# Weight transfers of the plain projections issued by GpSimd instead of SyncE, up to the last one in the gates' stage

## The chip, the cores and the metric

The kernel runs on one core of a Trainium2 chip. The metric is the device time of one execution, in microseconds (us). The engines of the core are named as in the profile: PE (TensorE, matrix products; PEld is its weight load), DVE (VectorE), ACT (ScalarE), POOL (GpSimd) and SP (SyncE). Each has its own queue of instructions and works through it in order. A DMA is put on the way by an instruction in the queue of one engine (in this kernel nearly always SP's, "SPq" in the profile) and then carried out by 16 DMA engines; the profile's DMA rows name the engine that issued it.

## The reference

One layer of a hybrid encoder block in float32, batch 1, 1024 tokens, width 1024. Cut to what matters:

```python
h = rms_norm(x)
proj = h @ w_in                      # q, k, v, r and gate codes of GLA; q, k, v of SWA; two branch gates
A = gla(q, k, v, r, gates) @ w_o_gla # gated linear attention, both directions, 4 heads, chunks
B = swa(q, k, v, sinks) @ w_o_swa    # windowed attention, 8 heads on 2 KV heads, blocks of 128
x = x + (sigmoid(gate_a) * A + sigmoid(gate_b) * B) @ w_out
h2 = rms_norm(x)
gate, up = split(h2 @ w_ffn_in)
x = x + (silu(gate) * up) @ w_ffn_out
```

## The kernel before, in words

Every product is made at nearly full float32 precision from operands that are split in two: a value's high part is its rounding to a shorter format (`h`, made by ACT), its low part what is left (`l`, a subtraction by DVE). A product then takes three matmuls: high by high, high by low, low by high. In the profile the split parts of the weights are `wh` and `wl`, those of the normalised input `xh` and `xl`, raw weights `wr`; accumulators of dense products are `mm`, those of the attention's small products `ch`.

A "unit" is a 128x512 piece of a weight, 256 KB. `wunit` loads it raw into `wr` (4 buffers), lets ACT make `wh` and DVE make `wl` (5 buffers each). The plain projections (all of `w_in` that is used as it stands: `w_f` for outputs with features on the partitions, `w_t` for outputs with tokens there) are generators of dense matmuls; each takes its units with `next_unit`, which keeps two more units ahead (`AHEAD = 2`) of the one in use. Half of the tokens are worked off in a first pass: `wkeep` loads a unit of `w_t`, splits it and stores the split parts to DRAM (for n < 2 only the low part, otherwise both), and `wagain` loads them again for the other half of the tokens: for n < 2 the raw unit, of which ACT makes `wh` anew, and the low part; otherwise both parts.

The order of work on PE is written out by hand. The attention's steps (gates, decays, scores, outputs of GLA; later scores and outputs of SWA) are set in slots, and `fill(n)` puts n dense matmuls between them, so that PE has work while a chain of small operations goes through ACT and DVE. The tables `GF` and `SF` say how many for each slot. The order on ACT, DVE, SP and POOL is not written out: a scheduler makes it, from the program's dependences and its own estimates of when each instruction can begin. So a change in one queue changes the order in the others.

Stages, by the profile's time: a start with the load of x, its split and the sums of the norm (to about 36 us); GLA with the projections filled in (to about 375 us); SWA likewise (to about 560 us); the products of the later layers, in which sums of quarters of the matrices are used (to the end). In the third of these the branch gates' projections are made in pairs (`pair_open`, `pair_T1`, ...), which begins while the last plain units are worked off. Sums of other weights (`w_ob`, `w_out`) are made by `prep` steps between GLA's slots: DVE adds two raw pieces `xn`, loaded by SP at line 618, and the sums (`bs...`, `wo...`) are stored to DRAM by SP at line 117.

Other names that the steps below use: `st` is a stage from which SP stores a projection's result (lines 152 and 237); `qk` and `vr` are reloads of q, k and v for a GLA chunk; `G` are gates (ACT lines 461 to 483, DVE lines 462 to 485); `th` and `tl` the split state of GLA (ACT line 557, DVE line 558); `ac` the split sum of squares of the norm (ACT line 133, DVE line 135), made of `acc` (DVE line 354); `sql` the low part of SWA's queries (line 833); `pl` the low part of its probabilities (line 890).

Of the kernel before, what the change touches and what calls it, by code (L numbers as in the profile page):

```python
# [8 lines left out]
F32 = mybir.dt.float32  # L9
# [21 lines left out]
def body(tc, i, out):  # L31
    nc = tc.nc
    with ExitStack() as root:
# [8 lines left out]
        def nm(s):  # L42
            uid[0] += 1
            return f"{s}_{uid[0]}"
# [13 lines left out]
        def load_const(pool, name, src, shape, dt=F32):  # L58
            t = pool.tile(list(shape), dt, tag=name, name=name)
            nc.sync.dma_start(out=t, in_=src)  # L60
            return t

        def wunit(src, n=512):
            raw = wp.tile([P, n], F32, tag="wr", name=nm("wr"), bufs=4)
            nc.sync.dma_start(out=raw, in_=src)
            h = wp.tile([P, n], FR, tag="wh", name=nm("wh"), bufs=5)
            nc.scalar.activation(h, raw, AF.Copy)  # L67
            l = wp.tile([P, n], FR, tag="wl", name=nm("wl"), bufs=5)
            nc.vector.tensor_tensor(l, raw, h.bitcast(F32), op=ALU.subtract)  # L69
            return h, l  # L70
# [96 lines left out]
        def wkeep(n, k):  # L167
            h, l = wunit(i["w_t"][n, k])
            kept[n, k] = []
            for v, q in ((h, "h"), (l, "l"))[n < 2:]:  # L170
                d = dram.tile([P, 512], F32, tag=f"w{q}{n}_{k}", name=f"w{q}{n}_{k}")
                nc.sync.dma_start(out=d, in_=v.bitcast(F32))
                kept[n, k].append(d)
            return h, l

        def wagain(n, k):
            r = []
            if n < 2:
                raw = wp.tile([P, 512], F32, tag="wr", name=nm("wr"), bufs=4)
                nc.sync.dma_start(out=raw, in_=i["w_t"][n, k])  # L180
                r.append(wp.tile([P, 512], FR, tag="wh", name=nm("wh"), bufs=5))
                nc.scalar.activation(r[0], raw, AF.Copy)
            for d, tag in zip(kept[n, k], ("wh", "wl")[n < 2:]):
                t = wp.tile([P, 512], FR, tag=tag, name=nm(tag), bufs=5)
                nc.sync.dma_start(out=t.bitcast(F32), in_=d)
                r.append(t)
            return r

# [84 lines left out]
        def fill(n):  # L273

            while n > 0 and dense:
                try:
                    next(dense[0])
                    n -= 1
                except StopIteration:
                    dense.pop(0)  # L280
# [659 lines left out]
        def xpart(q, k):  # L940
            r = xn.tile([P, HT], F32, tag="xn", name=nm("xn"))
            nc.sync.dma_start(out=r, in_=scr[f"x{q}", k])
            pool, th, tl, d = homes[q]
            XT[q].append(xsplit(pool, th.format(k + d), tl.format(k + d), r))
# [4 lines left out]
        for n in range(2 * KT):  # L949
            t, g = divmod(n, 2)  # L950
# [10 lines left out]
        with tc.manual_schedule(engines={mybir.EngineType.PE}):  # L961
            for t, v in enumerate(todo):
# [5 lines left out]
                if a_scores in names:  # L968
                    pin = a_turn in names and t < 5
                    k = names.index(a_turn) if pin else max(j for j, f in enumerate(names) if f is a_scores)  # L970
# [56 lines left out]
        def pair_open(f):  # L1027
            nme, m, a, b = PAIRS[f]
            g = pend[f] = Chunk()
            p1 = tp.tile([P, HT], F32, tag="np", name=nm("np"), bufs=2)  # L1030
            nc.sync.dma_start(out=p1, in_=scr[f"{nme}{m}", "p1"])
            g.X = mmtile()
            nc.scalar.copy(g.X, p1)
            g.r11, g.r21 = rawload(i["w_f"][a, 0], True), rawload(i["w_f"][b, 0], True)
            g.s = comb(g.r21, rawload(i["w_f"][b, 1], False), ALU.add)
            g.w = wsplit(g.s, 512)
# [102 lines left out]
        with tc.manual_schedule(engines={mybir.EngineType.PE}):  # L1139
            homes["T2"] = tp, "t2h{}", "t2l{}", 0  # L1140
            for k in range(4):
                if k == 2:
                    pair_open(0)
                xpart("T2", k)
                fill(8)
            while plan:
                fill(4)
            pair_open(1)
            fill(1 << 30)
            for f in range(2):  # L1150
                pair_T1(f)
            for q in ("T3", "T4"):
                for k in range(4):
                    xpart(q, k)
            for j in range(0, len(PAIRS), 2):
                two = (j, j + 1)
                for step in (pair_T2, pair_22):
                    for f in two:
                        step(f)
                v = [pair_T3(f) for f in two]  # L1160
                if j + 2 == len(PAIRS):
                    for f in two:
                        pair_w4(f)
                for f in two:
                    with tc.issue_after(v[f - j].ins):
                        for q, k in STEPS[f]:
                            parts[q](k)
                if j + 2 < len(PAIRS):
                    for f in two:
                        pair_open(f + 2)  # L1170
                    for f in two:
                        pair_T1(f + 2)
                for f in two:
                    if j + 2 < len(PAIRS):
                        pair_w4(f)
                    pair_T4(f)
# [591 lines left out]
```

## Time and profile before

| | |
|---|---|
| median of 3 runs | 1604.43 us (1604.23 to 1604.52) |
| the profiled execution: time, span | 1605.86 us, 1604.0 us |
| mean granted clock of PE | 0.999 |
| DMA moved | 349.47 MB, mean 218 GB/s |
| DMAs issued by SP and by POOL | 1421 and 0 |

Each row of a busy window has the stretch in us, its length, then busy us (and instructions) of PE, PEld, DVE, ACT and POOL, PE's granted clock as a share of full speed, the busy share of the 16 DMA engines, and GB/s. Each row of a timeline has the start, the duration, the engine, the line, the operation with output and input, and in brackets the idle time before it with what ended it. Each row of waits has the engine and its instruction, what it waited for, the total in us, how often, and the longest.

### The profile page before, as it was taken

How to read it: one execution, taken by the hardware profiler on the slowest of the kernel's cores; microseconds unless marked ns; L12 is line 12 of the kernel's file. 1: busy time of each engine (PE TensorE's matmuls, PEld its weight loads, DVE VectorE, ACT ScalarE, POOL GpSimd, SP SyncE). 2: the span in 40 equal slices, each digit the busy share in tenths (PEclk: the TensorE clock that was granted, in tenths of full speed). 3: DMA queues.
4: the chain of work that ended last, by engine and by line, in shares of the span. 5: the costliest groups of instructions: out<-in, count | busy, mean ns of one | idle time of the engine just before them, and what ended most of it. 6: DMA issues, size and time to landing. Idle time of an engine off the chain costs nothing.

```text
span 1604.0 us, 23251 instructions
## 1 busy us (share of the span) xinstructions
PE 1590.2 (99%) x7484; PEld 1322.5 (82%) x7484; DVE 1247.0 (78%) x2358; ACT 932.7 (58%) x1912; POOL 0.2 (0%) x4
## 2 busy tenths in 40 slices
PE   9999999999999999999999999999999999999999
PEld 7878888888888788888888888888888888888887
DVE  8577898846899877876887988777777878689655
ACT  7555877864998744545664647844444444354442
POOL 0000000000000000000000000000000000000000
PEclk9999999999999999999999999999999999999999
DMA  8877877888554799878876767634344564695433
GB/s 266 287 260 250 272 260 253 283 281 292 182 158 155 235 298 300 266 254 268 273 248 191 233 213 222 201 113 151 112 150 153 192 201 162 205 333 172 151 99 118
DMA packets 223900, 349.47 MB, mean 218 GB/s; under 512 B 24255, under 2 KB 67135, under 8 KB 223778
## 3 DMA queue, kind: packets, MB, share of 16 engines
q1 hardware_dynamic: 223778, 347.99, 66.6%
q8 instruction: 59, 0.97, 0.2%
q14 instruction: 63, 0.52, 0.1%
HBM read 235.17 MB, written 112.73 MB: 217 GB/s over the span
## 4 chain that ended last, share of the span: by engine, by line
PE 77%; DVE 11%; DMA 6%; ACT 3%; issue 2%; SPq 1%; DVEq 0%; ACTq 0%
PE mm L1013 10%; PE mm L1014 10%; PE mm L1012 10%; PE mm L73 8%; PE mm L1606 7%; PE ch L1606 6%; PE ch L1012 5%; PE ch L1013 5%; PE ch L1014 5%; PE ch L73 5%; PE mm L261 4%; DMA wr<-in_w_f_dram 1%; PE ch L886 1%; DVE wl L69 1%; DMA gb<-gb 1%
## 5 line engine op out<-in xcount | busy, mean ns | idle before, releaser
L991 ACT ACTIVATE wh<-ws 128x512 fp32r<-128x512 f32 x164 | 103.2, 631 | 150.6 <-PE mm L1013 74.7
L73 PE MATMUL mm<-wh,xl 128*128 128x512 f32 x320 | 127.2, 398 | 0.0
L73 PE MATMUL mm<-wl,xh 128*128 128x512 f32 x320 | 127.2, 397 | 0.0
L73 PE MATMUL mm<-wh,xh 128*128 128x512 f32 x320 | 127.0, 397 | 0.1
L992 DVE TENSOR_TENSOR wl<-ws,wh 128x512 fp32r<-128x512 f32 x164 | 112.0, 686 | 11.0 <-ACT wh L991 10.8
L991 ACT ACTIVATE wh<-a 128x512 fp32r<-128x512 f32 x66 | 41.8, 634 | 89.6 <-PE ch L1606 42.2
L991 ACT ACTIVATE wh<-wr 128x512 fp32r<-128x512 f32 x96 | 60.0, 629 | 45.0 <-PE mm L1013 13.9
L69 DVE TENSOR_TENSOR wl<-wr,wh 128x512 fp32r<-128x512 f32 x98 | 66.9, 685 | 15.3 <-ACT wh L67 15.3
L992 DVE TENSOR_TENSOR wl<-wr,wh 128x512 fp32r<-128x512 f32 x96 | 65.5, 686 | 15.3 <-ACT wh L991 15.3
L992 DVE TENSOR_TENSOR wl<-a,wh 128x512 fp32r<-128x512 f32 x66 | 45.5, 690 | 40.5 <-ACT wh L991 40.2
L67 ACT ACTIVATE wh<-wr 128x512 fp32r<-128x512 f32 x98 | 61.2, 629 | 23.0 <-PE mm L73 8.3
L73 PEld LDWEIGHTS mm<-wh,xh 128*128 128x128 f32 x320 | 60.2, 188 | 10.7 <-DVE st L148 0.6
L1606 PE MATMUL mm<-hh,wl 128*128 128x512 f32 x176 | 68.6, 390 | 0.0
L1606 PE MATMUL mm<-hl,wh 128*128 128x512 f32 x176 | 68.6, 390 | 0.0
L1606 PE MATMUL mm<-hh,wh 128*128 128x512 f32 x176 | 68.5, 389 | 0.0
L73 PEld LDWEIGHTS mm<-wl,xh 128*128 128x128 f32 x320 | 60.2, 188 | 9.7 <-DMA wl<-wl 0.2
L73 PEld LDWEIGHTS mm<-wh,xl 128*128 128x128 f32 x320 | 60.3, 188 | 8.9
L1005 DVE TENSOR_TENSOR ws<-wr,wr 128x512 f32<-128x512 f32 x80 | 54.6, 686 | 12.1 <-DMA wr<-in_w_out_dram 5.5
L1573 DVE TENSOR_TENSOR hl<-hr,hh 128x512 fp32r<-128x512 f32 x77 | 52.8, 686 | 5.2 <-ACT hh L1572 5.0
L1012 PE MATMUL mm<-S0h,wh 128*128 128x512 f32 x136 | 52.9, 389 | 0.0
L1013 PE MATMUL mm<-S0l,wh 128*128 128x512 f32 x136 | 52.9, 389 | 0.0
L1014 PE MATMUL mm<-S0h,wl 128*128 128x512 f32 x136 | 52.9, 389 | 0.0
(445 smaller groups left out, 4947.4 us busy)
## 6 DMA issues: line engine op xcount, KB each, us to landing
wr<-in_w_fi_dram SPq DMA_DIRECT2D x110, 256.0 KB, 3.9
wr<-in_w_f_dram SPq DMA_DIRECT2D x96, 256.0 KB, 3.9
wl<-wl SPq DMA_DIRECT2D x80, 256.0 KB, 3.4
wr<-in_w_t_dram SPq DMA_DIRECT2D x56, 256.0 KB, 3.6
wh<-wh SPq DMA_DIRECT2D x48, 256.0 KB, 3.5
B<-c SPq DMA_DIRECT2D x44, 256.0 KB, 2.0
T<-st SPq DMA_DIRECT2D x44, 256.0 KB, 3.0
a<-in_w_fo_dram SPq DMA_DIRECT2D x44, 256.0 KB, 5.3
```

Source lines behind the costliest of these rows:

```text
L67: nc.scalar.activation(h, raw, AF.Copy)
L69: nc.vector.tensor_tensor(l, raw, h.bitcast(F32), op=ALU.subtract)
L73: nc.tensor.matmul(o, a, b, start=start, stop=stop)
L261: nc.tensor.matmul(Y[q], w[:, c], x, start=f0, stop=f1, skip_group_check=True)
L991: nc.scalar.activation(h, src, AF.Copy)
L992: nc.vector.tensor_tensor(l, src, h.bitcast(F32), op=ALU.subtract)
L1005: nc.vector.tensor_tensor(t, x, y, op=op)
L1012: nc.tensor.matmul(o, h[:, c], x[kk][0], start=start and kk == 0, stop=False, skip_group_check=True)
L1013: nc.tensor.matmul(o, h[:, c], x[kk][1], start=False, stop=False, skip_group_check=True)
L1014: nc.tensor.matmul(o, l[:, c], x[kk][0], start=False, stop=kk == nk - 1, skip_group_check=True)
L1573: nc.vector.tensor_tensor(l, r, h.bitcast(F32), op=ALU.subtract)
L1606: nc.tensor.matmul(ys[m], a[:, c], b, start=f0, stop=f1, skip_group_check=True)
```

## The change: a second queue for the weights

A list of one, `via`, holds the engine that issues the weight transfers of the three functions. It is GpSimd from the beginning; behind the last plain unit, when the plan of projections has been worked off in the gates' stage, it is set to SyncE. Up to there 220 DMAs of 256 KB are issued by GpSimd: 76 raw loads in `wunit`, 64 stores of split parts in `wkeep`, 16 raw loads and 64 loads of split parts in `wagain`. The later uses of `wunit` (22 units) are issued by SyncE as before. Nothing else is edited.

```diff
+        via = [nc.gpsimd]
+
         def wunit(src, n=512):
             raw = wp.tile([P, n], F32, tag="wr", name=nm("wr"), bufs=4)
-            nc.sync.dma_start(out=raw, in_=src)
+            via[0].dma_start(out=raw, in_=src)
...
             for v, q in ((h, "h"), (l, "l"))[n < 2:]:
                 d = dram.tile([P, 512], F32, tag=f"w{q}{n}_{k}", name=f"w{q}{n}_{k}")
-                nc.sync.dma_start(out=d, in_=v.bitcast(F32))
+                via[0].dma_start(out=d, in_=v.bitcast(F32))
...
             if n < 2:
                 raw = wp.tile([P, 512], F32, tag="wr", name=nm("wr"), bufs=4)
-                nc.sync.dma_start(out=raw, in_=i["w_t"][n, k])
+                via[0].dma_start(out=raw, in_=i["w_t"][n, k])
...
             for d, tag in zip(kept[n, k], ("wh", "wl")[n < 2:]):
                 t = wp.tile([P, 512], FR, tag=tag, name=nm(tag), bufs=5)
-                nc.sync.dma_start(out=t.bitcast(F32), in_=d)
+                via[0].dma_start(out=t.bitcast(F32), in_=d)
...
             while plan:
                 fill(4)
             pair_open(1)
             fill(1 << 30)
+            via[0] = nc.sync
```

PE's order is the same before and after. The orders of DVE, ACT and SP change in many places. Line numbers are those of each kernel; after the edit they are higher by 2 from line 63 on. In the rows a tile's name carries numbers of its own.

SP, before, in GLA's second chunk pair: weight loads (`wr`, L65) and reloads of v (`vr`) stand among the sums' loads and stores, and the load of `xn_203_1210` behind two stores of q.

```order
L65 DMA wr_208_1245<-in_w_f_dram 128x512
L117 DMA bs4l_1_1106<-pwl_176_1101 128x512
L618 DMA xn_202_1208<-in_w_ob_dram 128x512
L117 DMA woh_1_1202<-pwh_199_1198 128x512
L65 DMA wr_234_1353<-in_w_f_dram 128x512
L502 DMA vr_237_1370<-v0_4_959 128x256
L502 DMA vr_237_1370<-v0_5_991 128x256
L65 DMA wr_249_1417<-in_w_f_dram 128x512
L117 DMA wol_1_1204<-pwl_200_1199 128x512
L152 DMA q1_0_1174<-st_192_1175 128x512
L152 DMA q1_1_1178<-st_193_1179 128x512
L618 DMA xn_203_1210<-in_w_ob_dram 128x512
```

SP, after, at the same place:

```order
L119 DMA bs4h_1_1104<-pwh_175_1100 128x512
L504 DMA vr_237_1370<-v0_4_959 128x256
L504 DMA vr_237_1370<-v0_5_991 128x256
L119 DMA bs4l_1_1106<-pwl_176_1101 128x512
L119 DMA woh_1_1202<-pwh_199_1198 128x512
L620 DMA xn_202_1208<-in_w_ob_dram 128x512
L119 DMA wol_1_1204<-pwl_200_1199 128x512
L620 DMA xn_203_1210<-in_w_ob_dram 128x512
L154 DMA q1_0_1174<-st_192_1175 128x512
L154 DMA q1_1_1178<-st_193_1179 128x512
```

The three weight loads are gone, the reloads of v stand earlier, and `xn_203_1210` is loaded ahead of the stores of q.

POOL, after, the same weight units (POOL issues no DMA before):

```order
L67 DMA wr_137_941<-in_w_f_dram 128x512
L187 DMA wl_113_841<-wl0_5_595 128x512
L187 DMA wl_116_859<-wl0_6_646 128x512
L67 DMA wr_140_947<-in_w_f_dram 128x512
L67 DMA wr_154_1017<-in_w_f_dram 128x512
L187 DMA wl_136_927<-wl0_7_666 128x512
L67 DMA wr_177_1110<-in_w_f_dram 128x512
L67 DMA wr_196_1184<-in_w_f_dram 128x512
L67 DMA wr_208_1245<-in_w_f_dram 128x512
L67 DMA wr_234_1353<-in_w_f_dram 128x512
```

The loads of `w_f` that were spread over SP's rows stand here one behind the other, between the second loads of `w_t`.

DVE, before, at the end of the start: the sums of squares `acc`, the low part `ac1` of their total, and the subtractions `wl` of the first weights.

```order
L354 TENSOR_TENSOR acc_136<-acc_136,sq_24_356 128x1024
L354 TENSOR_TENSOR acc_136<-acc_136,sq_25_359 128x1024
L354 TENSOR_TENSOR acc_136<-acc_136,sq_26_362 128x512 x2
L740 TENSOR_SCALAR kg_505<-kg_505 128x128
L135 TENSOR_TENSOR ac1_394<-acc_136,ac0_393 128x512
L69 TENSOR_TENSOR wl_45_517<-wr_43_513,wh_44_515 128x512
L135 TENSOR_TENSOR ac1_394<-acc_136,ac0_393 128x512
L69 TENSOR_TENSOR wl_48_525<-wr_46_521,wh_47_523 128x512
L69 TENSOR_TENSOR wl_51_533<-wr_49_529,wh_50_531 128x512
```

DVE, after, at the same place:

```order
L356 TENSOR_TENSOR acc_136<-acc_136,sq_24_356 128x1024
L71 TENSOR_TENSOR wl_45_517<-wr_43_513,wh_44_515 128x512
L356 TENSOR_TENSOR acc_136<-acc_136,sq_25_359 128x1024
L71 TENSOR_TENSOR wl_48_525<-wr_46_521,wh_47_523 128x512
L356 TENSOR_TENSOR acc_136<-acc_136,sq_26_362 128x512 x2
L71 TENSOR_TENSOR wl_51_533<-wr_49_529,wh_50_531 128x512
L137 TENSOR_TENSOR ac1_394<-acc_136,ac0_393 128x512 x2
L71 TENSOR_TENSOR wl_54_541<-wr_52_537,wh_53_539 128x512
```

Three subtractions of weights, which stood between and behind the two of `ac1`, stand between the sums of squares and ahead of `ac1`.

## The prediction

> **What bounds the kernel now.** I read the busy table first, then the windows by stage, then the waits of TensorE, then the places of those waits on the engines that feed it. The profiled execution took 1605.86 us, 1604.0 us of it the span, so 1.86 us lie around the span; it stands 1.43 us above the median of 1604.43 us. The sum below is made against 1605.86 and then lowered by 1.43.
>
> The busy table (busy us, share of the span, instructions) and two windows (busy us of PE, PEld, DVE, ACT, POOL; granted clock; DMA share; GB/s), from the end of the start-up to the attention stage, and that stage:
>
> ```profile
> PE 1590.2 (99%) x7484; PEld 1322.5 (82%) x7484; DVE 1247.0 (78%) x2358; ACT 932.7 (58%) x1912; POOL 0.2 (0%) x4
> 36.00:375.00 339.00, 334.33 (x1783) 281.71 (x1782) 254.90 (x576) 229.84 (x594) 0.00 (x0) 0.99 0.81 269
> 375.00:560.00 185.00, 182.71 (x981) 155.49 (x980) 163.29 (x461) 155.37 (x381) 0.00 (x0) 1.00 0.63 198
> ```
>
> TensorE bounds it: 99% busy, and the diff adds or removes no matmul. In the stretch that the change touches TensorE is idle for 339 − 334.33 + 185 − 182.71 = 6.96 us. That, and a lowered clock, is all that can be gained. TensorE's waits between 20 and 560 us (us in total, times, longest):
>
> ```profile
> PE ch L73 <- DVE pl L890: 1.9, 3, 0.8
> PE ch L73 <- ACT th L557: 1.7, 2, 1.0
> PE ch L73 <- ACT ac L133: 1.0, 2, 0.5
> PE ch L73 <- DVE tl L558: 1.0, 2, 0.7
> PE ch L73 <- DVE ob L587: 0.6, 1, 0.6
> PE ch L73 <- DVE sh L527: 0.5, 1, 0.5
> PE mm L73 <- ACT st L236: 0.4, 1, 0.4
> PE ch L73 <- DVE sql L833: 0.4, 1, 0.4
> PE ch L73 <- DVE sl L528: 0.2, 1, 0.2
> ```
>
> No line names a weight: TensorE never waits for wh, wl or a DMA here. The waits, 7.7 us in all, are for chains of small operations on ScalarE and VectorE. So moving weight transfers can only help where a late weight holds up one of these chains.
>
> **The change part by part.** SyncE's queue of DMAs runs in order, and weight transfers stand and wait in it. Its own waits in the same stretch, for the three moved lines:
>
> ```profile
> SPq L65 <- DVE wl L69: 28.7, 17, 7.2
> SPq L185 <- PE mm L73: 21.7, 17, 3.8
> SPq L172 <- DVE wl L69: 14.7, 16, 4.2
> ```
>
> These 65.1 us, and the issue time of 220 DMAs, leave SyncE. What stands behind them there is activation loads and stores, among them the xn, qk and vr loads. Conversely the raw loads no longer stand behind SyncE's other waits. What that is worth is read at the places where TensorE waits.
>
> *The stall at 112 us.* On TensorE (start, duration, idle before it and its releaser), and the windows there:
>
> ```profile
> 113.41 0.39 PE L73 MATMUL ch<-th,q2f 128*128 128x256 f32 x1 [0.99 <-ACT th L557]
> 114.46 0.39 PE L73 MATMUL ch<-tl,q2f 128*128 128x256 f32 x1 [0.67 <-DVE tl L558]
> 112.00:115.00 3.00, 1.34 (x8) 0.93 (x7) 2.56 (x6) 2.73 (x9) 0.00 (x0) 1.00 0.70 237
> 115.00:119.00 4.00, 4.00 (x12) 3.11 (x11) 3.75 (x9) 2.05 (x6) 0.00 (x0) 0.58 0.47 168
> ```
>
> 0.99 + 0.67 = 1.66 us idle, and behind it a stretch of 4 us at a granted clock of 0.58: (1 − 0.58) × 4 = 1.68 us more. Together 3.34 us hang on one chain. The Trainium skill ("TensorE: Matmul & The Clock Gate", Part 1) says that the clock halves after an idle window of about 3.4 us and returns after as long a busy one; here the trace shows the drop behind an idle time of only 1.66 us, so the row decides. The chain, back from its end: VectorE and ScalarE, then SyncE:
>
> ```profile
> 110.52 0.69 DVE L622 TENSOR_TENSOR xn<-xn,xn 128x512 f32<-128x512 f32 x1 [1.99 <-DMA xn<-in_w_ob_dram]
> 111.13 0.16 DVE L480 TENSOR_SCALAR G<-G 128x2 f32<-128x2 f32 x1
> 112.84 0.51 ACT L557 ACTIVATE th<-pf,dec 128x256 fp32r<-128x256 f32 x1
> 103.80 1.25 SPq L152 DMA_DIRECT2D q<-st x2
> 105.10 0.44 SPq L618 DMA_DIRECT2D xn<-in_w_ob_dram x1
> ```
>
> VectorE is in order: the gate's G (L480) stands behind the sum L622, which idles 1.99 us for an xn load that SyncE issued at 105.10, behind two q stores that began at 103.80. In the new order that load stands ahead of the two stores. So it can be issued about 105.10 − 103.80 = 1.30 us sooner, more if its queue has drained (three weight loads and their waits are gone from the dozen rows before it). Of th's 0.99 and tl's 0.67, which lie on the same chain one behind the other, an advance of 1.66 removes both. 1.30 alone would leave 0.36; with what the drained queue adds I take the full 1.66 and with it the 1.68 of the clock: −3.34. The ends: nothing (the load waits for its buffer anyway) and −3.34.
>
> *The waits at 85 and 92 us.* ScalarE and then TensorE:
>
> ```profile
> ACT wh L67 <- DMA wr<-in_w_f_dram: 8.2, 4, 4.0
> 82.88 0.63 ACT L67 ACTIVATE wh<-wr 128x512 fp32r<-128x512 f32 x1 [4.00 <-DMA wr<-in_w_f_dram]
> 85.24 0.50 PE L73 MATMUL mm<-xh,wh 128*128 128x512 f32 x1 [0.36 <-ACT st L236]
> 90.49 0.63 ACT L67 ACTIVATE wh<-wr 128x512 fp32r<-128x512 f32 x1 [2.10 <-DMA wr<-in_w_f_dram]
> 92.30 0.39 PE L73 MATMUL ch<-tl,q2f 128*128 128x256 f32 x1 [0.30 <-DVE tl L558]
> ```
>
> ScalarE idled 4.00 and 2.10 us for a raw w_f load, and evictions (st) and th stood behind it. On GpSimd's queue these loads no longer stand behind SyncE's stores of wo and xn. If the load comes 0.4 us sooner, 0.36 + 0.30 = 0.66 us go. I take −0.66, one end; the other is +0.66, since a wh that comes sooner also takes ScalarE from something else.
>
> *The other waits* (pl, ob, sh, sql, sl: 3.6 us in all): VectorE's order around them is changed, with no clear direction. I take −0.5, a seventh of them, for casts that ScalarE has done earlier; ends −3.6 and +3.6.
>
> *The start.* Raw loads of w_t come to stand in an empty queue, so the first four are issued as soon as their buffers are free, beside the loads of x. The scheduler answers by moving their casts and subtractions ahead of the norm's sums. Window of the start, then VectorE and TensorE:
>
> ```profile
> 4.00:24.00 20.00, 20.00 (x88) 16.77 (x88) 17.13 (x25) 18.09 (x27) 0.00 (x0) 1.00 0.98 327
> 28.77 1.29 DVE L354 TENSOR_TENSOR acc<-acc,sq 128x512 f32<-128x512 f32 x2 [0.52 <-DVE acc L354]
> 30.16 0.69 DVE L135 TENSOR_TENSOR ac<-acc,ac 128x512 fp32r<-128x512 f32 x1
> 30.18 0.50 PE L73 MATMUL ch<-ac,onesr 128*128 128x512 f32 x1 [0.45 <-ACT ac L133]
> ```
>
> Two wl subtractions of about 0.6 us (as long as the ac of 0.69) come into the chain of acc, which has 0.52 us of slack: 2 × 0.6 − 0.52 = +0.7, on the matmul that already waits at 30.18. The ends: 0 (the wh arrives too late to be taken first, and the order costs only a wait) and +1.8 (three subtractions, no slack). As to the transfers: 4 × 0.262 MB at 327 GB/s are 3.2 us in a stretch where the DMA share is 0.98 and TensorE is busy for 20.00 of 20.00. ScalarE (18.09) has 1.9 us of room, so I take +0.3, ends 0 and +3.2.
>
> *GpSimd's issue.* No DMA is issued by GpSimd in this trace, so its price is unknown. SyncE's rows for the same shape, and the moved DMAs in the densest stretch, 260 to 380 us (count, KB each, us to landing):
>
> ```profile
> L185 SPq DMA_DIRECT2D wl<-wl x40: 319/423/667, 49.5 to 412.5; - x40
> wh<-wh SPq DMA_DIRECT2D x34, 256.0 KB, 3.2
> wl<-wl SPq DMA_DIRECT2D x33, 256.0 KB, 3.3
> wr<-in_w_t_dram SPq DMA_DIRECT2D x15, 256.0 KB, 3.1
> wr<-in_w_f_dram SPq DMA_DIRECT2D x4, 256.0 KB, 3.8
> 260.00:380.00 120.00, 119.33 (x650) 101.17 (x649) 83.72 (x212) 86.02 (x244) 0.00 (x0) 1.00 0.85 282
> ```
>
> 34 + 33 + 15 + 4 = 86 DMAs in 120 us, one each 1.40 us. At SyncE's 0.42 us GpSimd would be busy for 36 us of 120; up to 1.4 us each the queue keeps up and the cost is nothing, hidden by two units of weights that are loaded ahead. Nearest row: 0.42, so I take 0; the far end is in the rivals. The Trainium skill ("DMA: Bandwidth & Descriptors", "Latency and other measured facts") gives a first byte after about 1 us from GpSimd against about 0.6 from SyncE; by that each landing would take an estimated 3.7 instead of 3.3 us, and the sum would be the same. No run here shows it yet. The bytes are the same and use the same 16 engines, whose share is 0.85 there, so nothing is gained in transfer.
>
> *Work that comes to wait.* On GpSimd a store that waits for wl holds the loads behind it, as it did on SyncE (14.7 us there); the loads have the units ahead as cover. If the cover is gone, wh is late for TensorE by the excess. The first scores of the attention stage wait for sql (0.4 above), and its subtraction now stands behind others: I take half of that, +0.2; ends −0.4 (the wait gone) and +1.4 (two subtractions of 0.69 ahead of it).
>
> Sum: −3.34 − 0.66 − 0.5 + 0.7 + 0.3 + 0.2 = −3.3. Then 1605.86 − 3.3 − 1.43 = 1601.1 us. Below 0.2% (3.2 us), a measurement of this kernel can hardly tell a difference from none; the forecast lies just beyond that line.
>
> **The rivals.**
>
> *The stall moves and nothing is gained.* The xn load waits for something other than SyncE's queue (its own buffer, freed by a sum on VectorE), or an engine as full as VectorE takes the time back: for it speaks that the DMA share is 0.7 to 0.85 throughout and that no weight is ever late for TensorE. Then the gain is 0.66 and the loss 0.7 + 0.3 + 0.2 = 1.2: 1604.43 + 0.5 = 1604.9, within 0.2%. A half gain, the 1.66 us without the clock, gives 1604.43 − 1.66 + 0.5 = 1603.3 and belongs here too.
>
> *GpSimd's issue is the bound (slower).* Place: 260 to 380 us. Point of decision: more than 1.40 us per DMA, waits counted. At 1.6 us the 86 take 137.6 us, 17.6 too long; the units loaded ahead hold some of it back, and taking half, +9: 1613. At 2.0 us it is 172 − 120 = 52, some 1650. Against it speaks SyncE's 0.42 us; for it, that nothing shows GpSimd issuing as fast. The Trainium skill ("SBUF — State Buffer", the "DVE blocks DMA" trap) says that descriptors of GpSimd's DMAs are written by GpSimd itself and cannot be while VectorE runs a copy, cast or tensor_scalar in its two-port mode. By that rule the trace's VectorE, 83.72 of 120 us busy there but mostly with TENSOR_TENSOR, would hold back few of them; no run here shows the lock.
>
> *The start and the attention stage pay (slower).* Place: the norm's sums at 30 us, where the far ends +1.8 and +3.2 add to 5.0 us, less 0.7 gained: 1604.43 + 4.3 = 1608.7. It decides from 3.2 us of loss with no gain at 112 us.
>
> **How the numbers follow.** Forecast (the chain at 112 us comes free): 0.44, all of it faster, 1596.0 to 1601.2; the best case is all 6.96 us of idle time and 1.68 of clock, 1604.43 − 8.64 = 1595.8. Stall moves: 0.28, all within 0.2%, 1601.2 to 1607.6. GpSimd bound: 0.15, slower. Start and attention pay: 0.13, slower. So faster 0.44, same 0.28, slower 0.28. For the range I leave out about 0.1 below (gains beyond 1597, which need all the waits gone) and about 0.1 above (an issue beyond 1.6 us each): 1597 to 1612. The likeliest case alone has 1598 to 1601.2.
>
> **What would show it.** Right: the wait for th and tl at 112 us gone, the clock at 1.0 between 115 and 119 us, ScalarE's idle time for wr in 60 to 125 us down from 8.2 us, POOL's DMA issues about 0.4 us each, TensorE's wait for ac near 30 us up by some 0.7. Wrong: a row of TensorE or its weight loads waiting for wh or wl, or ScalarE waiting longer for wr in 260 to 380 us (GpSimd is the bound); a new stretch of low clock anywhere; the wait for th still there with the xn load issued as late as before.

## The result, and the profile after

The changed kernel takes 1624.55 us (median of 4 runs, 1619.75 to 1624.98), the kernel before on the same chip 1604.47 us (4 runs, 1604.23 to 1605.02). The ratio is 1.0118, 95% interval 1.0104 to 1.0132: slower by about 19 us, where 1601.1 us was forecast and the range ended at 1612. Measured again later it gave 1.0115.

The profiled execution is the shortest of the four, 1619.75 us with a span of 1618.0 us. In the other three the mean granted clock was 0.995 to 0.996 instead of 0.999; 0.003 to 0.004 of 1620 us are 4.9 to 6.5 us, and they are longer by 4.6 to 5.2 us. So what follows explains 14.0 us of span, and the rest goes with a lower clock. A later profile of the same kernel (1626.88 us, span 1625.1 us, clock 0.995) shows where: besides the place near 96 us, which both have, its clock is lowered from 30 to 38 us (0.79), from 190 to 200 us (0.83) and from 400 to 412 us (0.86), where the first profile has 1.00. These are 1.7 us each, 5.1 us of the 7.1 by which its span is longer. The window of 190 to 200 us, first profile and later one:

```profile
190.00:200.00 10.00, 7.51 (x43) 6.41 (x44) 6.47 (x15) 5.67 (x15) 1.62 (x3) 1.00 0.58 190
190.00:200.00 10.00, 7.52 (x35) 6.23 (x34) 5.27 (x13) 4.46 (x13) 1.62 (x3) 0.83 0.78 244
```

TensorE stands idle equally long there, and the clock drops in one execution and not in the other.

The page of the kernel after, its busy table and its two main DMA queues (packets, MB, share of 16 engines):

```profile
PE 1592.6 (98%) x7484; PEld 1321.9 (82%) x7484; DVE 1248.1 (77%) x2358; ACT 931.5 (58%) x1912; POOL 119.3 (7%) x224
q1 hardware_dynamic: 192098, 290.30, 54.9%
q0 software_dynamic: 17600, 57.69, 11.1%
```

TensorE's idle time in the span was 1604.0 − 1590.2 = 13.8 us and is 1618.0 − 1592.6 = 25.4 us: 11.6 us of the 14.0. The other 2.4 us are longer matmuls with the same instructions: TensorE's busy time rose by that. GpSimd's 220 DMAs keep it busy for 119 us of 1618; it is nowhere near full.

The two stretches of the kernel after that were shown of before (busy us of PE, PEld, DVE, ACT, POOL; clock; DMA share; GB/s):

```profile
36.00:375.00 339.00, 327.91 (x1758) 276.74 (x1757) 248.30 (x557) 223.11 (x581) 85.99 (x159) 0.99 0.80 262
375.00:560.00 185.00, 180.74 (x958) 152.05 (x957) 163.71 (x464) 151.83 (x370) 25.35 (x48) 1.00 0.60 193
```

Idle time there went from 4.67 to 11.09 us and from 2.29 to 4.26 us, together from 6.96 to 15.35. TensorE's waits of the kernel after between 20 and 560 us (us in total, times, longest):

```profile
PE ch L75 <- ACT th L559: 4.4, 2, 3.7
PE ch L75 <- DVE sh L529: 3.1, 2, 2.6
PE ch L75 <- DVE pl L892: 2.0, 2, 1.5
PE ch L75 <- ACT ac L135: 1.2, 1, 1.2
PE ch L75 <- DVE kTl L819: 1.1, 2, 0.7
```

As before, no row names a weight. The same chains of small operations are waited for, but two single waits, 3.7 and 2.6 us, are longer than any of before (1.0).

The first stands at 95.7 us. The timeline of the kernel after, TensorE, ScalarE, VectorE and SyncE (start, duration, idle before and releaser):

```profile
95.67 0.51 PE L75 MATMUL ch<-th,q2f 128*128 128x256 f32 x1 [3.68 <-ACT th L559]
...
90.17 0.72 ACT L465 ACTIVATE G<-G,ones 128x512 f32<-128x512 f32 x1 [6.75 <-DVE G L464]
...
87.90 0.69 DVE L624 TENSOR_TENSOR xn<-xn,xn 128x512 f32<-128x512 f32 x1 [2.45 <-DMA xn<-in_w_ob_dram]
...
89.71 0.42 DVE L464 TENSOR_SCALAR G<-G 128x512 f32<-128x512 f32 x1
...
84.91 0.48 SPq L620 DMA_DIRECT2D xn<-in_w_ob_dram  x1
```

VectorE stands 2.45 us for an xn load issued at 84.91, and the gate's G, on which th depends, stands behind the sum. It is the shape of the stall that the prediction read at 112 us, at another place. But this is no new place in VectorE's order. In the kernel before the same sum and the one after it stand ahead of the same G too, and the same load was issued 7.8 us earlier:

```profile
82.24 0.69 DVE L622 TENSOR_TENSOR xn<-xn,xn 128x512 f32<-128x512 f32 x1 [4.40 <-DMA qk<-k]
85.85 0.42 DVE L462 TENSOR_SCALAR G<-G 128x512 f32<-128x512 f32 x1
77.10 0.42 SPq L618 DMA_DIRECT2D xn<-in_w_ob_dram  x1
```

So here the loads come later, and with them G, by 3.9 us (85.85 and 89.71). By the trace, part of this is SyncE's new order: between 71 and 79 us three reloads of v and a pair of q and k now stand ahead of the sums' stores and loads, and SyncE waits 4.9 us at the reloads of v. Part is older: the sum before is already 5.1 us later (64.56 and 69.66). No run takes the two apart. The second stall, at 192.4 us, does come from a new place, that of a product:

```profile
192.39 0.36 PE L75 MATMUL ch<-vh,sh 128*128 128x256 f32 x1 [2.63 <-DVE sh L529]
...
191.29 0.75 DVE L629 SCALAR_TENSOR_TENSOR xn<-xn,g,rstd 128x512 f32<-128x512 f32 x1 [3.82 <-DMA xn<-in_xT_dram]
191.96 0.28 DVE L529 CAST sh<-sp 128x256 fp32r<-128x256 f32 x1
...
187.24 0.43 SPq L620 DMA_DIRECT2D xn<-in_xT_dram  x1
```

In the kernel before, the order of VectorE has the same product behind sh:

```profile
186.19 0.29 DVE L527 CAST sh<-sp 128x256 fp32r<-128x256 f32 x1
187.12 0.75 DVE L627 SCALAR_TENSOR_TENSOR xn<-xn,g,rstd 128x512 f32<-128x512 f32 x1
```

And at 112 us the forecast came true:

```profile
112.00:115.00 3.00, 3.00 (x18) 2.60 (x17) 2.56 (x7) 2.25 (x6) 0.54 (x1) 1.00 0.36 135
115.00:119.00 4.00, 4.00 (x25) 3.52 (x24) 3.43 (x8) 2.47 (x8) 0.00 (x0) 1.00 0.50 164
96.00:100.00 4.00, 3.78 (x12) 2.98 (x12) 3.31 (x8) 3.02 (x8) 0.17 (x1) 0.60 0.92 313
```

No idle time and a full clock from 112 to 119 us. The low clock has moved along with the stall: 0.60 from 96 to 100 us, behind the idle 3.68 us.

GpSimd's issues in the kernel after (busy us, mean ns of one; idle before them and releasers):

```profile
L67 POOL DMA_DIRECT2D wr<-in_w_t_dram x40 | 21.8, 545 | 54.2 <-DVE wl L379 13.9 <-DVE wl L71 11.7 <-DVE G L464 7.8
L187 POOL DMA_DIRECT2D wl<-wl x40 | 21.5, 538 | 72.6 <-PE mm L75 71.7 <-issue 0.3
```

### The profile page after: what moved, and what is told of

It reads as the page before. It is cut to its first block, busy times and chain, and to the rows that moved or that the text cites. A ratio compares the mean times of both kernels' runs of the same rounds, so it can differ in the third digit from the quotient of the medians.

```text
span 1618.0 us, 23369 instructions
## 1 busy us (share of the span) xinstructions
PE 1592.6 (98%) x7484; PEld 1321.9 (82%) x7484; DVE 1248.1 (77%) x2358; ACT 931.5 (58%) x1912; POOL 119.3 (7%) x224
## 4 chain that ended last, share of the span: by engine, by line
PE 78%; DVE 10%; DMA 7%; ACT 3%; issue 2%; SPq 0%; POOL 0%; ACTq 0%; DVEq 0%; POOLq 0%
PE mm L1014 10%; PE mm L1015 10%; PE mm L1016 10%; PE mm L75 7%; PE mm L1609 7%; PE ch L1609 6%; PE ch L1014 6%; PE ch L1015 5%; PE ch L1016 5%; PE ch L75 5%; PE mm L263 4%; DVE G L466 1%; DMA xn<-in_w_ob_dram 1%; DMA qr<-sq 1%; DVE wl L71 1%
## 5 line engine op out<-in xcount | busy, mean ns | idle before, releaser
L994 DVE TENSOR_TENSOR wl<-wr,wh 128x512 fp32r<-128x512 f32 x96 | 65.5, 685 | 13.8 <-ACT wh L993 13.7
```

Of the source, the lines that this page charges most:

```text
L994: nc.vector.tensor_tensor(l, src, h.bitcast(F32), op=ALU.subtract)
```

## The experiments

The change does two things. The issuer moves, and the scheduler answers by another order on VectorE, ScalarE and SyncE. To take them apart, the program is built twice. The first build gives an order for each engine, and the second, with another issuer, is held to it by edges that set the order and add no wait. In the expectations theory A says that the new orders cost the time (A1 and A2: that of one engine), B that the issuer does, C that GpSimd's earlier start does, D that the second queue itself does, and E that SyncE's changed pace does (for the moved instructions E is used in another sense, given there). The order is set up to the last plain unit; behind it the scheduler is free, but the traces of the two kernels with GpSimd in the old order and SyncE in the new one show VectorE and ScalarE in the order they were to have there too, by line and tile name. The lines common to these kernels, in short form; what stands behind # here and in the edits is a remark of this text:

```
def build(weights, order=None, engines=()):       # via = [getattr(nc, weights)]
    ...
    follow(tc, traced, {e: [n for n in names if mine[n] == e] for e in engines}, engines)
order = build("sync")[2]                          # the kernel before's order
nc, arrays, _ = build("gpsimd", order, (ET.DVE, ET.Activation, ET.SP, ET.Pool))
```

**The issuer alone, and the order alone.** First, as printed above, GpSimd issues and every engine keeps its old order. Then the reverse:

> GpSimd issues the same 220 DMAs as in the changed kernel, but the instructions of VectorE, ScalarE and PE are kept in exactly the order of the kernel before, SP's and GpSimd's DMAs in the order that they had in SP's one queue. Theory A (the loss of 20 us is the new order on VectorE and ScalarE): 1601 to 1607 us, the wait of sh at 192 us (2.6) and of th at 96 us (3.7) gone. Theory B (the loss is GpSimd's issue itself, 0.54 us against 0.42, and its later landing, 4.1 us against 3.4 for wl): 1617 to 1626 us, as the changed kernel.

```
-    order = build("sync")[2]
-    nc, arrays, _ = build("gpsimd", order, (ET.DVE, ET.Activation, ET.SP, ET.Pool))
+    order = build("gpsimd")[2]
+    nc, arrays, _ = build("sync", order, (ET.DVE, ET.Activation, ET.SP))
```

> The mirror: SP issues all DMAs again, but VectorE, ScalarE and SP keep the order of the changed kernel, its GpSimd DMAs merged into SP's queue at the place where the scheduler sent them. Theory A: 1616 to 1628 us, with waits of PE for sh and th as in the changed kernel. Theory B: 1603 to 1608 us.

Measured: the issuer alone 1613.75 us, ratio 1.0051 (1.0032 to 1.0070), about 8 us slower, and 1.0051 when measured again (below). The order alone 1622.10 us, ratio 1.0105 (1.0081 to 1.0128), about 17 us slower, though SyncE issues everything as before. TensorE's waits with the issuer alone, and then with the order alone, 20 to 560 us:

```profile
PE ch L75 <- ACT th L559: 2.5, 3, 1.6
PE ch L75 <- DVE pl L892: 1.9, 2, 1.7
PE ch L75 <- ACT ac L135: 1.6, 2, 1.0
```

```profile
PE ch L75 <- ACT th L559: 5.1, 2, 4.2
PE ch L75 <- DVE sh L529: 2.1, 2, 1.6
```

The two long waits go with the new order, not with the issuer. The first time, 1613.75, lies between the ranges of theories A and B: neither is the whole. Both parts cost, and they don't add up: 8 and 17, but 19 together.

With the issuer alone one more row appears that neither the kernel before nor the changed one has: TensorE waits for a weight, wl, 0.4 us here and 1.1 us when the kernel was measured again. So weights come late for it there, by little.

**Parts of the change.** The 76 raw loads of `wunit` alone on GpSimd, and then all others (stores, second loads and the 16 raw loads that go with them), with the scheduler free:

> Only wunit's 76 raw loads are issued by GpSimd; stores and second loads of the split parts stay with SP, and the scheduler orders the rest. VectorE's order then differs from before in far fewer places (some 30 against 180). Theory A: 1602 to 1608 us. Theory B, by 76 of 220 DMAs: about 1611 us.

```
-                via[0].dma_start(out=d, in_=v.bitcast(F32))
+                nc.sync.dma_start(out=d, in_=v.bitcast(F32))
...
-                via[0].dma_start(out=raw, in_=i["w_t"][n, k])
+                nc.sync.dma_start(out=raw, in_=i["w_t"][n, k])
...
-                via[0].dma_start(out=t.bitcast(F32), in_=d)
+                nc.sync.dma_start(out=t.bitcast(F32), in_=d)
```

> Only wkeep's 64 stores and wagain's 80 loads are issued by GpSimd; wunit's raw loads stay with SP. VectorE's order differs from before in about as many places as in the changed kernel. Theory A: 1614 to 1626 us. Theory B, by 144 of 220 DMAs: about 1617 us. If both single parts cost nothing, the loss needs both queues to be emptied at once.

```
         def wunit(src, n=512):
-            via[0].dma_start(out=raw, in_=src)
+            nc.sync.dma_start(out=raw, in_=src)
```

Measured: 1612.14 us, 1.0047 (1.0031 to 1.0063), above the range that theory A gave, and 1622.25 us, 1.0108 (1.0087 to 1.0129). Neither half is free. The second has nearly the whole loss, and the same two waits as the full change.

**The term of −3.34 by itself.** In the kernel before, SyncE issuing, one load moves ahead of the two q stores:

> The kernel before, with all DMAs issued by SP and every engine's order kept, but for one row: the load of xn_203_1210 stands ahead of the two stores of q in SP's queue. It prices the largest term of the prediction by itself. If that term was right: 1600.5 to 1602 us, PE's wait of 1.66 us at 112 us and the low clock behind it gone. Rival (the load would not have landed sooner, or the stores of q that now stand behind it make another chain late): 1603.5 to 1606 us.

```
+    order = build("sync")[2]
+    order.remove("I-1211")                                 # load of xn_203_1210
+    order.insert(order.index("I-1177"), "I-1211")          # ahead of the first store of q
+    nc, arrays, _ = build("sync", order, (ET.DVE, ET.Activation, ET.SP, ET.Pool))
```

Its windows at that place:

```profile
112.00:115.00 3.00, 2.33 (x15) 1.88 (x14) 2.56 (x6) 2.76 (x8) 0.00 (x0) 1.00 0.98 301
115.00:119.00 4.00, 4.00 (x21) 3.30 (x21) 3.75 (x8) 1.84 (x6) 0.00 (x0) 1.00 0.43 160
```

Idle time there fell from 1.66 to 0.67 us and the clock rose from 0.58 to 1.00, so 0.99 + 1.68 = 2.7 us were won on the spot. The time was 1607.08 us beside 1605.67, ratio 1.0007 (0.9997 to 1.0016): nothing was won in all. In this profile TensorE's idle time from 36 to 375 us is 5.55 us beside 4.67, so more than the 0.99 came back at other places of the same stretch. And the 1.68 us of clock weren't there to be won each time: in 9 of the 17 executions of the kernel before that stand beside this one the granted clock was 1.000, which leaves no room for such a stretch (it takes 0.1% off the mean); with the load moved it was 1.000 in 4 of 12. This kernel is also the control for the method: with all four engines held to a written order, and one load moved, the time is within 0.16% of the kernel before.

**One engine's old order.** GpSimd issues; only VectorE, or only SyncE and GpSimd, is held to the old order:

> GpSimd issues the 220 DMAs; VectorE alone keeps the order of the kernel before, ScalarE, SP and GpSimd are ordered by the scheduler around it. Theory A1 (of the new orders it is VectorE's that costs): as with all old orders, 1609 to 1616 us. Rival A2 (ScalarE's or SP's new order costs as much): 1616 to 1625 us.

> GpSimd issues the 220 DMAs; SP's and GpSimd's DMAs keep the order of the kernel before, VectorE and ScalarE are ordered by the scheduler. Theory A1: near the changed kernel, 1616 to 1626 us, since VectorE's order differs from before in some 130 places. Rival A2 (the order of the loads and stores costs, above all xn's): 1608 to 1615 us.

```
-    nc, arrays, _ = build("gpsimd", order, (ET.DVE, ET.Activation, ET.SP, ET.Pool))
+    nc, arrays, _ = build("gpsimd", order, (ET.DVE,))            # one
+    nc, arrays, _ = build("gpsimd", order, (ET.SP, ET.Pool))     # the other
```

Measured: 1627.09 us, 1.0134 (1.0119 to 1.0150), and 1633.07 us, 1.0180 (1.0157 to 1.0203). The first isn't told from the changed kernel (1.0118, 1.0104 to 1.0132), the second is slower than it. Both times lie above every range that was given for them. And the pair doesn't say which engine's new order carries the loss: with one engine held, the scheduler gave the others a third order, neither that of before nor that of after (with VectorE held, TensorE waits 5.0 us in one piece for a wl, which it does in neither of the two).

**The new order with three instructions moved.** The two xn sums at 88 us go behind G, where they don't stand in the kernel before either, and the product at 191 us goes back behind sh and sl:

> The changed kernel with three instructions of VectorE moved: the xn sums that stand ahead of the gates' G at 88 to 90 us go behind it, and the xn product at 191 us behind sh and sl. PE waited there 3.7 us for th and 2.6 us for sh. Theory E (the new order costs because sums whose loads land late stand ahead of the gates): 1612 to 1619 us, 6 to 12 us less than the changed kernel, with the low clock behind the stalls. Rival (the stall only moves to the next chain): 1620 to 1626 us.

```
+    order = build("gpsimd")[2]
+    for n, behind in (("I-910", "I-982"), ("I-969", "I-1046"), ("I-2346", "I-2269")):
+        order.remove(n)
+        order.insert(order.index(behind) + 1, n)
```

> The changed kernel itself, on the same chip as the experiments: 1620 to 1627 us. It is the base for the two others of this set.

Measured: 1622.33 us, 1.0102 (1.0082 to 1.0121), against the unaltered changed kernel's 1623.07 us, 1.0115 (1.0092 to 1.0138), on the same chip. The intervals overlap. TensorE's waits in the kernel with the three moved, 20 to 560 us:

```profile
PE ch L75 <- ACT th L559: 3.2, 2, 2.7
PE mm L75 <- ACT st L238: 2.2, 1, 2.2
PE ch L75 <- DVE pl L892: 1.8, 2, 1.3
PE ch L75 <- ACT kb L548: 1.6, 2, 1.1
```

The wait for sh has fallen from 3.1 to 0.5 us, and waits of 2.2 and 1.6 us for st and kb stand at the head instead. G comes 3.1 us sooner (86.62 instead of 89.71), but the longest wait for th falls only from 3.7 to 2.7 us. The stall was in part shortened and in part moved.

**Where the issuer costs.** All orders old, GpSimd issuing only up to the attention stage:

> All old orders again with GpSimd issuing, but SP takes the weights back at the start of the attention stage (about 375 us) and not in the gates' stage. With all old orders and GpSimd to the end PE lost 3.7 us more than before between 500 and 600 us. If that is the price of a second queue beside SP's in that stage: 1607 to 1611 us, about 4 us less than the median of 1613.75. If it was chance: 1612 to 1616 us.

```
+        via[0] = nc.sync
         order = (prep, a_rope, a_scores, a_turn, k_turn, a_out, a_probs)
```

Measured: 1612.30 us, 1.0043 (1.0028 to 1.0057). That is 7 of the 8 us; what the attention stage adds isn't told from nothing.

**Is it the earlier start?** On its own queue a weight DMA can run ahead of SyncE's stores. Here each waits for the operation that made what SyncE's last store ahead of it stores:

> All old orders, GpSimd issuing to the end, as the first experiment (1613.75 us), but each DMA of GpSimd waits for the operation that made what SP's last store ahead of it, in the old order of one queue, stores. So a weight transfer no longer starts before the stores that stood ahead of it could start. Theory C (with equal orders the cost of the second queue is that weights start sooner and take the DMA engines from SP's small urgent loads, which land 1 us later): 1603 to 1609 us. Theory D (the cost is GpSimd's path itself, whenever it starts): 1612 to 1617 us.

```
+        elif i.engine == mybir.EngineType.Pool and n in source and last:
+            tc.add_manual_dep(i, last, Sync, "hold")
```

Measured: 1614.24 us, 1.0051 (1.0037 to 1.0066), the same as unheld. Here TensorE waits 2.9 us for weights (wh 2.0, loads of wl and wh 0.6 and 0.3) beside 0.4 unheld, so holding costs some us itself. The earlier start isn't most of the 8 us; that it is none of them isn't shown.

**Is it GpSimd's kind of queue, and its room?** The 76 raw loads alone, all orders old, issued by ScalarE and by GpSimd; then all of GpSimd's DMAs with half the room for descriptors:

> The 76 raw loads of wunit are issued by ScalarE, the rest by SP, all old orders. A second queue without GpSimd, though ScalarE, which works in order, now waits for buffers too. Theory D1 (GpSimd's own path makes SP's small loads late): landings as before, 2.1 us for o, 2.9 for the qk of q, 3.4 for the raw w_t. Theory D2 (any second queue does): 2.8 to 3.3, 3.5 to 4.2 and 4.0 us or more. The time itself may go up by ScalarE's waits: 1606 to 1625 us.

> The same 76 raw loads issued by GpSimd, the rest by SP, all old orders: the other half of the pair. 76 of 220 DMAs: 1606 to 1612 us. D1: landings of SP's small loads a third of the way to those of the first experiment or more, o 2.5 to 3.2 us, the qk of q 3.3 to 4.1 us. D2: the same as with ScalarE.

```
     # stores and second loads: nc.sync
-    nc, arrays, _ = build("gpsimd", order, (ET.DVE, ET.Activation, ET.SP, ET.Pool))
+    nc, arrays, _ = build("scalar", order, (ET.DVE, ET.Activation, ET.SP, ET.Pool))
```

> All old orders, GpSimd issuing all 220 DMAs, as the first experiment, with half the room for GpSimd's descriptors (512 instead of 1024 bytes a partition; more than 1024 does not fit beside the tiles). If that room limits GpSimd's DMAs: issues longer than 0.54 us, landings over 4.2 us, 1618 us or more. If not: 1611 to 1617 us with the same rows.

```
-        nc = _bacc.Bacc("TRN2", target_bir_lowering=False, num_devices=1, dynamic_dma_scratch_size=1024)
+        nc = _bacc.Bacc("TRN2", target_bir_lowering=False, num_devices=1, dynamic_dma_scratch_size=512)
```

Measured: by ScalarE 1609.52 us, 1.0031 (1.0022 to 1.0041); by GpSimd 1609.28 us, 1.0028 (1.0016 to 1.0041). Moving these loads to a second queue costs 4 to 5 us with either issuer. That it is the same cause in both isn't shown: ScalarE's 76 issues at 0.335 us are also 25 us of an engine that has work of its own. The landings, 36 to 375 us, ScalarE's kernel and then GpSimd's:

```profile
wr<-in_w_t_dram ACTq DMA_DIRECT2D x33, 256.0 KB, 3.7
wr<-in_w_f_dram ACTq DMA_DIRECT2D x16, 256.0 KB, 3.6
```

```profile
wr<-in_w_t_dram POOLq DMA_DIRECT2D x33, 256.0 KB, 3.7
wr<-in_w_f_dram POOLq DMA_DIRECT2D x16, 256.0 KB, 4.2
```

The loads of w_t land equally late, those of w_f 0.6 us later from GpSimd, and SyncE's stores of o land after 2.6 us beside ScalarE's queue and after 3.3 beside GpSimd's. So neither of the theories D1 and D2 holds as it was stated.

With half the room 1617.48 us, 1.0087 (1.0063 to 1.0111); its GpSimd rows:

```profile
L187 POOL DMA_DIRECT2D wl<-wl x40 | 21.6, 539 | 47.6 <-issue 27.6 <-PE mm L75 18.6 <-PE ch L608 0.4
...
L187 POOL DMA_DIRECT2D wh<-wh x24 | 12.9, 539 | 25.7 <-PE mm L75 10.4 <-issue 7.0 <-PE ch L888 4.0
```

Here GpSimd stands 27.6 us at the issues of this line for nothing that the profile shows, against 0.3 us with the full room, in the old order too. So with the full room it isn't short. Half the room makes weights late: TensorE waits 5.2 us for them (wh 2.0, wl 1.8, loads of wl 1.4).

**Is it SyncE's own pace?** Without the weights' waits (28.7, 21.7 and 14.7 us before) SyncE issues its loads in another rhythm. In one kernel both queues are held as if they were one; in another only SyncE's DMAs are held; the unheld one runs beside them:

> GpSimd issues the weight DMAs, every engine keeps the order of the kernel before, and the two queues wait for each other's work as if they were one: a DMA of GpSimd waits for what made the source of SyncE's last store ahead of it, and a DMA of SyncE waits for what the weight DMAs ahead of it wait for (a weight just split, a weight buffer just read). Theory E (pacing): the 8 us that the second queue cost come from SyncE no longer being held back by the weights' waits, so that its loads are issued in denser bunches; then this kernel stands within 3 us of the kernel before, and the 64 KB loads of o land in 2.1 to 2.5 us. Theory D (two queues, whatever their pacing, lengthen the landings): again 7 to 11 us slower than the kernel before, with o's landing at 3.0 us or more.

> As the kernel in which both queues are held, but only SyncE's DMAs are held: each waits for what the weight DMAs ahead of it wait for; GpSimd runs ahead as it likes. Theory E (pacing of SyncE): within 3 us of the kernel before, o lands in 2.1 to 2.5 us. Theory D (two queues as such): 7 to 11 us slower, o at 3.0 us or more. If this one is slow and the one with both held is not, it is the two leads together.

```
+        # a DMA of GpSimd notes in held what it waits for: the maker of its source, the last readers of its buffer
+        elif i.engine == mybir.EngineType.SP:
+            for h in held:
+                tc.add_manual_dep(i, h, Sync, "hold")
```

> The kernel in which GpSimd issues and every engine keeps its old order, once more, as the measure for the two held ones on the same chip. All theories: 7 to 10 us slower than the kernel before, ratio 1.0045 to 1.0065, o's 64 KB loads landing in 3.2 us.

Measured: both held 1617.93 us, 1.0077 (1.0057 to 1.0097); SyncE held 1616.92 us, 1.0079 (1.0050 to 1.0108); unheld 1613.54 us, 1.0051 (1.0033 to 1.0069). The pacing theory falls: held back, the time doesn't come down, and o still lands after 3.4 us in both.

**The landings.** Beside a second queue SyncE's DMAs land later. (o<-ot are stores of GLA's output, though the expectations call them loads.) Issues between 36 and 375 us (count, KB each, median us to landing), first of the kernel before, then of GpSimd issuing in the old order:

```profile
xn<-in_xT_dram SPq DMA_DIRECT2D x16, 256.0 KB, 3.4
o<-ot SPq DMA_DIRECT2D x64, 64.0 KB, 2.1
qk<-q SPq DMA_DIRECT2D x16, 128.0 KB, 2.9
```

```profile
xn<-in_xT_dram SPq DMA_DIRECT2D x16, 256.0 KB, 4.3
o<-ot SPq DMA_DIRECT2D x64, 64.0 KB, 3.2
qk<-q SPq DMA_DIRECT2D x16, 128.0 KB, 4.1
```

The same DMAs, issued by the same engine in the same order, land 0.9 to 1.2 us later. The row of o, by kernel, with the ratio:

| kernel | o lands after, us | ratio |
|---|---|---|
| before | 2.1 | 1 |
| xn load first (SyncE) | 2.3 | 1.0007 |
| raw loads by ScalarE, old order | 2.6 | 1.0031 |
| raw loads by GpSimd, old order | 3.3 | 1.0028 |
| raw loads by GpSimd, order free | 3.5 | 1.0047 |
| GpSimd, old order | 3.2 | 1.0051 |
| the same, GpSimd held / both held | 3.2 / 3.4 | 1.0051 / 1.0077 |
| SyncE, new order | 2.9 | 1.0105 |
| GpSimd, only SyncE and GpSimd in the old order | 3.1 | 1.0180 |
| after | 3.6 | 1.0118 |

The landing isn't the whole of it. The two kernels with the raw loads in the old order have 2.6 and 3.3 and one time, and the new order alone has 2.9 with a single queue. Other landings move without a second queue and without loss: with the one xn load moved, xn<-in_xT lands after 4.0 us instead of 3.4 and qk<-q after 3.5 instead of 2.9, at a ratio of 1.0007.

How a later landing reaches VectorE can be followed at one place. The third xn sum waits for the landing of a store of bs by SyncE; the kernel before, GpSimd in the old order, and after:

```profile
59.17 0.69 DVE L622 TENSOR_TENSOR xn<-xn,xn 128x512 f32<-128x512 f32 x1 [1.19 <-DMA bs<-xn]
60.97 0.69 DVE L624 TENSOR_TENSOR xn<-xn,xn 128x512 f32<-128x512 f32 x1 [1.92 <-DMA bs<-xn]
62.63 0.69 DVE L624 TENSOR_TENSOR xn<-xn,xn 128x512 f32<-128x512 f32 x1 [3.69 <-DMA bs<-xn]
```

The fourth sum then waits 4.70, 5.77 and 6.34 us for its load and begins at 64.56, 67.43 and 69.66 us; it stands ahead of a G in both orders. With the raw loads alone on GpSimd these two waits are 1.00 and 4.25 us, no longer than before; with SyncE issuing in the new order they are 3.27 and 6.16 us. With GpSimd in the old order TensorE's wait for th behind this, at 92.5 us, is 0.2 us. So later landings do make these sums late, but here TensorE hardly pays for it in the old order. Where it pays the 8 us isn't shown.

## Why the prediction was wrong, point by point

**"GpSimd's issue … I take 0": the step that failed first.** On the issue itself the reasoning held: it takes 0.54 us, where 0.42 of SyncE's rows was taken and 1.40 was the point of decision, and no weight is late for TensorE in the changed kernel. So the slower rival "GpSimd's issue is the bound", which gave 1613, had the sign and not the mechanism. What was missing is a price for the two queues. "The bytes are the same and use the same 16 engines, so nothing is gained in transfer" stops half way: something is lost. With every order kept it measured +8 us, 7 of them ahead of the attention stage. Holding GpSimd's starts or SyncE's pace back doesn't take it away, and ScalarE as issuer costs as much for the 76 raw loads, with its own issue time as a second possible cause. VectorE isn't slowed by GpSimd's work either: its busy time is 1247.0 us before and 1247.8 with the issuer alone. That the later landings carry the loss is an inference: they make VectorE's sums late at 59 to 70 us, but across kernels they don't go with the loss in size. What makes the landings longer stays open.

**"The other waits … I take −0.5": the step that failed most.** The prediction saw that VectorE's order changes and set ends of ±3.6 us around waits that already stood in the trace. The new orders brought waits that weren't there: 3.7 us where xn sums stand ahead of G, as before, but their loads now come later, with a low clock behind it; 2.6 us where a product now stands ahead of sh; and others up to 560 us. With SyncE issuing, the new order costs 17 us. The shape was known, since the prediction had read it at 112 us ("VectorE is in order: the gate's G stands behind the sum"). It was priced there and not at the other places where a load's user stands ahead of a gate. Yet no single row accounts for the 17 us: with three of them moved the time isn't told from the changed kernel's, and which engine's order counts for how much stays open. Part of the loss is clock: over the five executions with the new order alone it averages 0.997, beside 0.9994 for the kernel before, which is 0.24% of the 1.05%.

**"−3.34" at 112 us: right in place, wrong as a term of the sum.** In the kernel after both parts are gone, the wait and the low clock. Alone, in the kernel before, the same move won 2.7 us on the spot and 0 in all (1.0007). A wait removed was counted as time saved; here other waits of the same stretch grew, which is the first rival ("the stall moves"), given 0.28. The 1.68 us of clock were also taken from one execution. In the five later sets of runs, on four chips, the kernel before ran with a clock of 1.000 in 38 of 68 executions, so it lacked that stretch in more than half. The prediction took off 1.68 for it and another 1.43 because the profiled execution was longer than the median; if the stretch was the reason for the 1.43, it was counted twice. The clocks of the three executions behind that median aren't known, so this stays a possibility.

**"−0.66" at 85 and 92 us.** The cause was right: between 60 and 125 us ScalarE's idle time for raw w_f, 8.2 us, is no longer among its waits of 0.5 us or more. The gain isn't to be seen, since the new stall of 3.68 us stands in the same stretch.

**The start, +0.7 and +0.3.** TensorE's wait for ac rose from 1.0 to 1.2 us, so +0.2; the right place at a third of the size. The wait for sql, for which +0.2 was taken, is no longer among TensorE's waits; the other end, −0.4, came true. The third rival (the start and the attention stage pay) has no share in the loss beyond that and the attention stage's 1 us, which isn't told from nothing.

**The estimates from the Trainium skill.** By the first bytes that its page "DMA: Bandwidth & Descriptors", section "Latency and other measured facts", gives (about 1 and 0.6 us), the prediction estimated each landing of GpSimd's as 0.4 us longer. With ScalarE (in SyncE's place) and GpSimd as issuers and one order, the w_t loads land after 3.7 us from both and the w_f loads after 3.6 and 4.2, so one row shows no such difference and the other one of 0.6; the runs don't decide. The lock that the Trainium skill's page "SBUF — State Buffer" describes under "DVE blocks DMA" doesn't show in the issues: the longest of GpSimd's took 0.68 us, with VectorE busy for 77% of the span. Whether it has a share in the later landings, no run tests.

**What stays open.** Why two queues lengthen the landings. Why the issuer's 8 us and the order's 17 don't add up. Which rows of the new order make its 17 us. And when the clock drops behind a short wait, since it does so in one execution of a kernel and not in another.

No version was faster than the kernel before.

## What to carry to other kernels

When a change lets a scheduler write a new order, go through the whole difference on each in-order engine and mark every place where an operation that waits for a load stands ahead of one that feeds TensorE. Look at the places where it has newly come ahead, and at the old ones where the load behind it is now issued later. The new order alone cost 17 us here, where the forecast gain was 3.3. Moving transfers to a second queue isn't free when bytes and engines are the same: look at how long the first queue's small transfers take to land and at what depends on them. And where waits form one long chain, try the removal of a single wait by itself before counting it: here 2.7 us won on the spot were 0 at the end. If part of the price is a lowered clock, see first in how many executions it is lowered.

## What the runs showed of the hardware

- A 256 KB DMA cost GpSimd 0.54 us to issue (536 to 679 ns) and ScalarE 0.335. SyncE took 0.42 for the raw loads that were moved, and 0.33 for those of a later weight (`w_fi`, behind 920 us).
- The same 76 raw loads, 19.93 MB, went in 6080 packets from GpSimd's queue (3.3 KB each) and in 10944 from ScalarE's (1.8 KB each); they took 4.7% and 4.2% of the 16 engines' time.
- The granted clock fell to 0.58 to 0.60 over 4 us behind idle stretches of 1.66 us (in two pieces) and of 3.68 us. Behind one of 2.63 us it stayed at 1.00 in one execution of the changed kernel; behind the wait at the same place, 2.5 us, it fell to 0.83 over 190 to 200 us in another.
